# Modulation steps moved from two out-projections into the gMLP's u half, a PSUM bank held for a pair, a weight read moved ahead

## The chip, the cores and the metric

The kernel runs on one core of one Trainium2 chip. The metric is the device time of one execution in microseconds; less is better. A core has TensorE (PE, matmuls; PEld is its weight load), VectorE (DVE), ScalarE (ACT), GpSimd (POOL) and SyncE (SP, which here only issues DMAs). Each engine, and SP, works its instructions off in program order and waits on semaphores for the others.

## The reference

Two layers over 512 latent tokens and 256 context tokens, width 1024. Each layer is FFN, mixer, FFN; the mixer of the first layer is a chunked gMLP, that of the second is attention. Every sub-layer has shift, scale and gate vectors from a modulation of the conditioning, and ends in a layer norm.

```python
def modulation(cond, w_mod, b_mod):
    m = jax.nn.silu(cond) @ w_mod + b_mod
    return jnp.split(m[..., None, :], N_MOD, axis=-1)          # N_MOD = 9

def ffn_sublayer(x, shift, scale, gate, w_in, w_out, ln_g, ln_b):
    y = swiglu(modulate(x, shift, scale), w_in, w_out)
    return layer_norm(ALPHA * x + 0.5 * gate * y, ln_g, ln_b)

def gmlp_mix(h, w_in, sgu_g, sgu_b, w_s, b_s, w_out):
    b_, t_, _ = h.shape
    u, v = jnp.split(jax.nn.gelu(h @ w_in, approximate=False), 2, axis=-1)
    v = layer_norm(v, sgu_g, sgu_b)
    v = v.reshape(b_, t_ // CHUNK, CHUNK, GMLP_GROUPS, GMLP_HALF // GMLP_GROUPS)
    v = jnp.einsum('gpq,bnqgc->bnpgc', w_s, v) + b_s.T[None, None, :, :, None]
    return (u * v.reshape(b_, t_, GMLP_HALF)) @ w_out
```

## The kernel before

**Stages.** The six sub-layers run one after another; every one of the first five ends in an out-projection during which the next one's input is prepared. Times in the profiled execution: first FFN's gated products to 372 us, its out-projection to 554 and its end to some 580; the gMLP's v half to 754, its u half to 982, its out-projection to 1171; second FFN to 1679, third FFN to 2191, then attention and the last FFN.

**Products.** Operands are split into a high and a low part and each product takes three matmuls. Weights come by SP into six `raw` buffers; ScalarE rounds them to the high part, VectorE subtracts for the low part (`w`, eight buffers). The gated products and u use a Strassen scheme: seven products (B11, T1, T2, B21, T3, B22, T4; 12 matmuls each) for a pair of output chunks, partly added up by VectorE (`sums`). A product's end is a *slot*: `step` issues the product, then `slot` flushes the low parts that wait, prepares two more weight units (`pump`), runs a modulation step if asked to (`fills`), and then the evacuations (`post`).

**The u half** (`gmlp`). The twelve pairs are a loop over `a`. Its PSUM banks are four (`part_bank`); four more go round for the spatial products (`mix_bank`). The bank called `seeded` takes B11's copy, then T2, T3 and T4; after T4 ScalarE reads it in `gelu(x, seeded)`, behind two other GELUs. `b1` takes B11 and B21, `b2` takes T1 and B22. `bank()` gives out the bank that was given out longest ago and is not held. v is written to DRAM in the v half, read back chunk by chunk (`fetch`), normalised by ScalarE (`normed`) and multiplied by the group's spatial weights (`spatial`); VectorE scales the result into S (`mixed`) and multiplies it with u (`times`), one or two such jobs a slot from the list `late`. The products then go to DRAM by POOL (`act<-stage`) and come back for the out-projection (`q<-act`, by `feed` and `prepare`). `load_ws` reads a group's spatial weights.

**The modulation.** A unit (layer, i) is one of the nine vectors. It takes 16 steps (two halves of 512 columns by eight blocks of rows). A step (`fill`) is two instructions of VectorE (`acc<-mraw,cs,acc`, latent and context) on a 256 KB block of w_mod that SP loaded into one of three `mraw` buffers. After each half POOL sums over the partitions (`PARTITION_ALL_REDUCE`, L476) and adds the row to a DRAM vector (`mod<-acc`, L477), both conditions one after the other. When a shift and its scale are there, `mod_columns` reads them back (`s<-mod`) three steps later and has TensorE transpose them (`ps<-ident,s`) three steps after that; gates are read straight (`gate<-mod`). `MOD_PLAN` says in which sub-layer a unit's steps run; what is left at the end of an out-projection is drained there.

**The out-projection** (`out_proj`) goes through the chunks twice, once for each half of 512 output columns: 22 chunks in an FFN, 24 in the gMLP, 18 matmuls a chunk. Each chunk's slot has a weight unit, the next chunk's activations, and one or more `fill`s, whose rate `x % 8` and `acts.ring` (true in the gMLP) set. `residual` gives the jobs that bring the old stream into z; in the first sub-layer it is six plain loads. At the end each block of tokens is normalised: statistics on VectorE, the power -1/2 on POOL (L204), the scaling on ScalarE (L2239), transposes on TensorE.

The order of the work is the program order of these functions; when `pin` is on, VectorE and ScalarE keep it exactly.

Of the kernel before, what the change touches and what calls it, by code (L numbers as in the profile page):

```python
# [13 lines left out]
P = 128  # L14
# [12 lines left out]
GMLP_CH = GMLP_HALF // P  # L27
GMLP_GROUPS = 8
# [41 lines left out]
MOD_PLAN = [  # L70
    [(0, 2), (0, 3), (0, 4), (0, 5), (0, 6)],
    [(0, 7), (0, 8)],
    [(1, 0), (1, 1), (1, 2)],
# [21 lines left out]
class Backbone:  # L95
# [788 lines left out]
    def out_proj(self, acts, l, i, factor, end, prev, gate_at=2):  # L884
# [9 lines left out]
        for half, order in enumerate(orders):  # L894
            body = n - CLOSE * half
            for x in range(body):
# [22 lines left out]
                if adds:  # L919
                    if x:  # L920
                        b, z, tmp = adds.pop(0)
                        self.dve.tensor_tensor(z, z, tmp, ALU.add)
                        self.dve.bn_stats(st[b][:, 0], z)
                    self.fill(int(prev is None or self.light))
                elif residual and x > 2 and (half or x % 2):
                    residual.pop(0)()
                    self.fill(int(self.light or acts.ring and x % 4 == 1))
                elif half or x < n - 1:
                    self.fill_pair()
                    if prev is None and x % 8 in (1, 3, 6) or acts.ring and x % 8 in (2, 6):  # L930
                        self.fill()
# [494 lines left out]
    def gmlp(self, l, i, nblocks, end, prev):  # L1426
# [3 lines left out]
        vst = [self.const.tile([P, CC, 6], F32, name=f"vst{b}") for b in range(NB)]  # L1430
        room = self.box("v", F32)
        self.gmlp_v(room, spill, vst)
        dve, act = self.dve, self.act

        acts = Acts(self, GMLP_CH, TOK, KEPT_MIX, READ_BACK_MIX, f"act{l}{i}_")
# [5 lines left out]
        T1, T2 = slice(0, HT), slice(HT, TOK)  # L1441
        ws_raw = {}

        for x in range(4):
# [8 lines left out]
        def load_ws(g):  # L1453
            if g < GMLP_GROUPS:
                wg = ws_raw[g] = self.sm([P], "w_s")
                self.sp.dma_start(wg, io["gmlp_w_s"][0, g])

# [94 lines left out]
        nothing = lambda: None  # L1552
        load_ws(0)
        load_ws(1)
# [3 lines left out]
        for a in range(0, GMLP_CH, 2):  # L1558
            begin, final = not a, a == GMLP_CH - 2
            seeded = self.part_bank(marked=True)  # L1560
            b1, g = self.part_bank(), self.acc()[:, 0:HT]
            step(b1, "B11", False, lambda: act.copy(seeded, b1), v_stats if begin else lambda: normed(a))
            if begin:
                next(self.following)
            if final:
                self.filler_raw()
            b2, p5 = self.part_bank(), self.acc()[:, 0:HT]
            step(b2, "T1", False, None, lambda: act.copy(p5, b2), v_bias if begin else nothing)
            if final:
                acts.prepare(0, 0)  # L1570
            v, w = self.q(512)[:, 0:HT], self.q(512)[:, 0:HT]
            half = (lambda j, x: lambda: normed(j, range(HALF * x, HALF * x + HALF))) if begin else lambda j, x: nothing
            step(seeded, "T2", True, None, lambda: act.copy(v, seeded), half(0, 0))
            if final:
                acts.prepare(0, 1)
            step(b1, "B21", True, None, lambda: gelu(g, b1), half(0, 1))
            if begin:
                self.grp_next = next(self.following)
            else:
                spatial(a)  # L1580
                late.append(lambda: times(a, T1, g))
# [7 lines left out]
            if final:  # L1589
                acts.prepare(0, 2)  # L1590

# [4 lines left out]

            step(seeded, "T4", True, None, last)
            if begin:
# [742 lines left out]
```

## Time and profile before

| | us |
|---|---|
| three runs | 2809.52, 2812.65, 2814.51 (median 2812.65) |
| the profiled execution | 2813.58 |
| its span (first to last instruction) | 2811.8 |

| stage | us from the span's start | VectorE busy |
|---|---|---|
| first FFN, gated products with steps | 215 to 358 | 130.1 of 143.0 |
| its out-projection, four windows | 371.7 to 554 | 148.7 of 182.3 |
| u, eight pairs | 814.6 to 964.3 | 103.0 of 149.7 |

A row of the timeline has the start, the length, engine, line, operation, output and inputs, count, and in brackets the idle time of that engine before it with what ended it. L90 is the line of the wrapper through which most instructions are issued, so operations are told apart by the names of their tiles.

### The profile page before, as it was taken

The numbers are of one execution on the slowest core, as the hardware profiler recorded it, in microseconds if no ns is written. First come the engines' busy times: TensorE is split into PE (matmuls) and PEld (weight loads), VectorE is DVE, ScalarE is ACT, GpSimd is POOL, SyncE is SP. The second block draws the span as 40 slices with busy tenths as digits, with TensorE's granted clock in tenths as the row PEclk, the third lists the DMA queues.
The fourth block names the chain that finished last, engine by engine and source line by source line (L and its number), as shares of the span: only waits on it lengthen the run. The fifth ranks groups of instructions, "written<-read, shape, count | busy, mean of one in ns | idle before, by whom it ended". The sixth has DMA issues, their size and how long they took to land.

```text
span 2811.8 us, 40725 instructions
## 1 busy us (share of the span) xinstructions
PE 2737.7 (97%) x14234; PEld 2464.8 (88%) x14234; DVE 2086.1 (74%) x3554; ACT 1314.4 (47%) x2624; POOL 555.8 (20%) x627
## 2 busy tenths in 40 slices
PE   7999998999999999999999999999999999999998
PEld 5999986788899987899999889999988888888887
DVE  6879988777776687687898658789886598733445
ACT  6544432275566631474444237444432666623321
POOL 1002145312100143300223220013242121000001
PEclk9999999999999999999999999999999999999999
DMA  7444475457644584444546534454595524454352
GB/s 232 141 141 140 137 242 184 153 176 234 208 148 155 163 268 147 140 147 141 147 140 219 178 108 134 141 154 137 164 311 161 147 72 86 129 151 134 113 169 86
DMA packets 408134, 448.09 MB, mean 159 GB/s; under 512 B 29624, under 2 KB 289144, under 8 KB 407928
## 3 DMA queue, kind: packets, MB, share of 16 engines
q1 hardware_dynamic: 371416, 331.99, 38.2%
q0 software_dynamic: 36512, 113.51, 13.3%
q8 instruction: 111, 1.82, 0.3%
q14 instruction: 95, 0.78, 0.1%
HBM read 383.40 MB, written 64.19 MB: 159 GB/s over the span
## 4 chain that ended last, share of the span: by engine, by line
PE 78%; DVE 6%; issue 5%; ACT 4%; DMA 4%; POOL 3%; SPq 0%; DVEq 0%; POOLq 0%; ACTq 0%
PE ps L90 77%; POOL acc L476 2%; DVE acc L90 1%; DVE w L90 1%; DMA mraw<-in_w_mod_dram 1%; ACT w L90 1%; DMA q<-act 1%; PE pp L90 1%; DVE acts L90 1%; DMA raw<-in_w_mod_dram 1%; ACT z L2239 1%; DVE z L90 0%; DVE q L90 0%; ACT h L694 0%; DMA acc<-in_gmlp_w_in_dram 0%
## 5 line engine op out<-in xcount | busy, mean ns | idle before, releaser
L90 PE MATMUL ps<-comb,w 128*128 128x384 f32 x6552 | 1156.1, 336 | 11.4 <-ACT acc L90 5.8
L90 PEld LDWEIGHTS ps<-comb,w 128*128 128x128 f32 x6552 | 1137.8, 188 | 18.4 <-ACT acc L90 9.0
L90 PE MATMUL ps<-w,acts 128*128 128x512 f32 (+1 forms) x3792 | 867.7, 390 | 10.2 <-DVE q L90 8.1
L90 PEld LDWEIGHTS ps<-w,acts 128*128 128x128 f32 x3792 | 711.2, 189 | 158.7 <-DVE q L90 9.0
L90 ACT CAST w<-raw 128x512 fp32r<-128x512 f32 x643 | 397.7, 621 | 622.5 <-PE ps L90 520.0
L90 DVE TENSOR_TENSOR w<-raw,w 128x512 fp32r<-128x512 f32 x643 | 471.3, 738 | 284.7 <-ACT w L90 283.0
L90 DVE SCALAR_TENSOR_TENSOR acc<-mraw,cs,acc 128x512 f32<-128x512 f32 x392 | 277.7, 743 | 27.9 <-DMA mraw<-in_w_mod_dram 27.6
L476 POOL PARTITION_ALL_REDUCE acc<-acc x56 | 208.0, 3720 | 339.1 <-DVE acc L90 305.2
L90 PE MATMUL ps<-h,w 128*128 128x512 f32 (+1 forms) x1152 | 241.4, 372 | 0.2 <-DVE w L174 0.2
L90 POOL DMA_DIRECT2D act<-stage x86 | 48.1, 559 | 953.9 <-DVE stage L90 935.6
L90 PEld LDWEIGHTS ps<-h,w 128*128 128x128 f32 x1152 | 203.2, 188 | 37.7 <-DVE w L174 0.4
L90 DVE TENSOR_TENSOR w<-sums,w 128x512 fp32r<-128x512 f32 x234 | 165.3, 711 | 69.2 <-ACT w L90 69.0
L90 POOL DMA_DIRECT2D q<-act x234 | 134.1, 638 | 405.3 <-DVE acts L90 270.5
L90 ACT COPY q<-ps 128x384 f32<-128x384 f32 (+1 forms) x206 | 99.4, 483 | 237.3 <-PE ps L90 237.2
L90 ACT CAST acts<-q 128x384 fp32r<-128x384 f32 (+1 forms) x270 | 132.0, 520 | 98.2 <-DMA q<-act 80.4
L90 PE MATMUL ps<-w,comb 128*128 128x512 f32 x756 | 173.2, 390 | 0.4 <-DVE w L90 0.2
L90 DVE TENSOR_TENSOR acts<-q,acts 128x384 fp32r<-128x384 f32 (+1 forms) x270 | 160.2, 628 | 14.6 <-ACT acts L90 14.3
L90 PEld LDWEIGHTS ps<-w,comb 128*128 128x128 f32 x756 | 141.4, 188 | 30.9 <-DVE w L90 1.0
L90 ACT CAST w<-sums 128x512 fp32r<-128x512 f32 x234 | 144.8, 620 | 45.2 <-DVE sums L355 23.3
L90 DVE TENSOR_TENSOR q<-q,ps 128x384 f32<-128x384 f32 (+1 forms) x81 | 46.1, 570 | 58.7 <-PE ps L90 58.6
L204 POOL TENSOR_TENSOR rs<-ve,mhalf 128x1 f32<-128x1 f32 (+3 forms) x47 | 38.6, 821 | 249.3 <-DVE ve L201 139.6
L174 DVE TENSOR_TENSOR w<-raw,w 128x512 fp32r<-128x512 f32 x101 | 67.1, 687 | 25.2 <-ACT w L173 24.6
(208 smaller groups left out, 2491.3 us busy)
## 6 DMA issues: line engine op xcount, KB each, us to landing
raw<-in_ffn_w_in_dram SPq DMA_DIRECT2D x400, 256.0 KB
mraw<-in_w_mod_dram SPq DMA_DIRECT2D x256, 256.0 KB
raw<-in_ffn_w_out_dram SPq DMA_DIRECT2D x176, 256.0 KB
q<-act POOLq DMA_DIRECT2D x224, 192.0 KB, 4.6
raw<-in_gmlp_w_in_dram SPq DMA_DIRECT2D x132, 256.0 KB
act<-stage POOLq DMA_DIRECT2D x76, 384.0 KB, 3.2
zhat<-z POOLq DMA_DIRECT2D x26, 512.0 KB, 3.0
raw<-in_gmlp_w_out_dram SPq DMA_DIRECT2D x48, 256.0 KB
```

The costliest lines, as they stand in the source:

```text
L90: return self.tc.keep_in_program_order(f(*args, **kwargs))
L174: self.lows.append((key, lambda: self.dve.tensor_tensor(lo, src, hi.bitcast(F32), ALU.subtract)))
L204: self.last_rstd = self.nc.gpsimd.tensor_tensor(rs, ve, self.mhalf[:, 0:1].to_broadcast([P, n]), ALU.pow).ins
L476: nc.gpsimd.partition_all_reduce(accs[c], accs[c], P, bass_isa.ReduceOp.add)
L2239: k.act.activation(k.z[b], k.z[b], AF.Identity, bias=nb, scale=rs)
```

## The change

Unit (0, 6) moves from the first sub-layer's plan to the gMLP's. In the out-projection the extra steps are fewer: in the first sub-layer one extra at x % 8 == 3 instead of three in eight, in the gMLP none. In u, ten of the twelve pairs run a step in the slots of T1, B21 and B22, and three of those pairs one more in T4's. The bank of T4 is held until T4's slot is over (`part_bank("mixed")`, `unhold`). The temporaries g, p5 and x come from `q` and no longer from `acc`, which the modulation uses. The first group's spatial weights are read ahead of the v half. In the last pair the reads of the first activations for the out-projection are spread over three places.

```diff
 MOD_PLAN = [
-    [(0, 2), (0, 3), (0, 4), (0, 5), (0, 6)],
-    [(0, 7), (0, 8)],
+    [(0, 2), (0, 3), (0, 4), (0, 5)],
+    [(0, 6), (0, 7), (0, 8)],
...
                 elif residual and x > 2 and (half or x % 2):
                     residual.pop(0)()
-                    self.fill(int(self.light or acts.ring and x % 4 == 1))
+                    self.fill(int(self.light))
                 elif half or x < n - 1:
                     self.fill_pair()
-                    if prev is None and x % 8 in (1, 3, 6) or acts.ring and x % 8 in (2, 6):
+                    if prev is None and x % 8 == 3:
                         self.fill()
...
+        load_ws(0)
         self.gmlp_v(room, spill, vst)
...
-        def step(ps, name, go_on, early, *posts):
+        def step(ps, name, go_on, early, *posts, fills=0):
...
-            self.slot(post, 2, 0, early)
+            self.slot(post, 2, fills, early)
...
-        load_ws(0)
+        temp = lambda: self.q(512)[:, 0:HT]
         load_ws(1)
...
-            seeded = self.part_bank(marked=True)
-            b1, g = self.part_bank(), self.acc()[:, 0:HT]
+            seeded = self.part_bank("mixed", marked=True)
+            b1, extra = self.part_bank(), int(not begin and a < GMLP_CH - 2)
             step(b1, "B11", False, lambda: act.copy(seeded, b1), v_stats if begin else lambda: normed(a))
+            b2, p5 = self.part_bank(), temp()
+            step(b2, "T1", False, None, lambda: act.copy(p5, b2), v_bias if begin else nothing, fills=extra)
...
             if final:
-                self.filler_raw()
-            b2, p5 = self.part_bank(), self.acc()[:, 0:HT]
-            step(b2, "T1", False, None, lambda: act.copy(p5, b2), v_bias if begin else nothing)
-            if final:
                 acts.prepare(0, 0)
-            v, w = self.q(512)[:, 0:HT], self.q(512)[:, 0:HT]
+                acts.feed(0, 1)
+            v = temp()
...
-            step(b1, "B21", True, None, lambda: gelu(g, b1), half(0, 1))
+            g = temp()
+            step(b1, "B21", True, None, lambda: gelu(g, b1), half(0, 1), fills=extra)
...
-            if a >= GMLP_CH - 4:
-                acts.feed(0, 2)
+            w = temp()
             step(seeded, "T3", True, lambda: act.copy(w, seeded), half(1, 0) if begin else lambda: normed(a + 1))
-            step(b2, "B22", True, None, lambda: add(v, v, b2), lambda: add(w, w, p5), half(1, 1))
-            if not begin:
+            if final:
+                acts.prepare(0, 1)
+                acts.feed(0, 1)
+            step(b2, "B22", True, None, lambda: add(v, v, b2), lambda: add(w, w, p5), half(1, 1), fills=extra)
+            if begin:
+                self.filler_raw()
+            else:
                 spatial(a + 1)
-            x = self.acc()[:, 0:HT]
-            if final:
-                acts.prepare(0, 2)
+            if a == GMLP_CH - 4:
+                acts.feed(0, 1)
+            x = temp()
...
-            step(seeded, "T4", True, None, last)
+            step(seeded, "T4", True, None, last, fills=int(extra and a % 8 == 4))
+            self.unhold("mixed")
```

**How instructions move: SP in the first sub-layer's out-projection.** First the order before, at the place where the gate (`mod_1910`) and the columns of units (0, 3) and (0, 4) (`s_4470` from `mod_2930` and `mod_3862`) are read:

```order
L90 DMA mraw<-in_w_mod_dram 128x512 x2
L90 DMA raw<-in_ffn_w_out_dram 128x512
L90 DMA gate<-mod_1910 128x1024 x2
L90 DMA s_4470<-mod_2930 8x128
L90 DMA s_4470<-mod_3862 8x128
L90 DMA mraw<-in_w_mod_dram 128x512
```

The same place in the changed kernel, where the columns' tile is `s_4565`:

```order
L90 DMA gate<-mod_1910 128x1024 x2
L90 DMA mraw<-in_w_mod_dram 128x512
L90 DMA raw<-in_ffn_w_out_dram 128x512
L90 DMA mraw<-in_w_mod_dram 128x512
L90 DMA raw<-in_ffn_w_out_dram 128x512
L90 DMA mraw<-in_w_mod_dram 128x512
L90 DMA raw<-in_ffn_w_out_dram 128x512
L90 DMA s_4565<-mod_2930 8x128
L90 DMA s_4565<-mod_3862 8x128
```

The columns' read stood right behind the gate's two reads and now stands three chunks further on. In TensorE's order the transposes of these columns move with it, from behind 270 matmuls of the out-projection to behind 342.

**POOL at the end of the same sub-layer.** `mod_4852` is unit (0, 6) before; `mod_4453` in the change is unit (0, 5); `act_2` to `act_7` are the reads for the second pass, and L204 is the power for the closing layer norm:

```order
 L90 DMA q<-act_2_966 128x384 x2
 L90 DMA q<-act_3_967 128x384 x2
-L476 ISA acc<-acc 128x512
-L477 DMA mod_4852<-acc 16x1x32
-L476 ISA acc<-acc 128x512
-L477 DMA mod_4852<-acc 16x1x32
 L90 DMA q<-act_4_968 128x384 x2
 L90 DMA q<-act_5_969 128x384 x2
 L90 DMA q<-act_6_970 128x384 x2
 L90 DMA q<-act_7_971 128x384 x2
-L476 ISA acc<-acc 128x512
-L477 DMA mod_4852<-acc 16x1x32
-L476 ISA acc<-acc 128x512
-L477 DMA mod_4852<-acc 16x1x32
 L204 ISA
```

The last all-reduces stood directly ahead of L204; now none stands behind the read of act_2.

**VectorE in a pair of u.** Before, from the scaled bias (`s_`) of a pair's first spatial product, behind B21, to the additions behind B22 (`q<-q,ps`); `S` is the scaled spatial product, `w` a low part:

```order
L90 SCALAR_TENSOR_TENSOR s_7974<-S,sguT 128x128
L90 TENSOR_TENSOR w<-raw,w 128x512
L90 TENSOR_TENSOR w<-sums,w 128x512 x2
L355 TENSOR_TENSOR sums<-raw,sums 128x512
L90 TENSOR_TENSOR w<-raw,w 128x512
L90 SCALAR_TENSOR_TENSOR S<-ps,sguT,s_7974 128x384 x2
L90 TENSOR_TENSOR w<-raw,w 128x512
L336 TENSOR_TENSOR sums<-raw 128x512
L90 TENSOR_TENSOR q<-q,ps 128x384
L90 TENSOR_TENSOR q<-q,acc 128x384
```

The same stretch of a pair in the change:

```order
L90 SCALAR_TENSOR_TENSOR s_9165<-S,sguT 128x128
L90 TENSOR_TENSOR w<-sums,w 128x512 x2
L90 SCALAR_TENSOR_TENSOR acc<-mraw,cs,acc 128x512 x2
L90 TENSOR_TENSOR w<-raw,w 128x512
L90 SCALAR_TENSOR_TENSOR S<-ps,sguT,s_9165 128x384 x2
L355 TENSOR_TENSOR sums<-raw,sums 128x512
L90 SCALAR_TENSOR_TENSOR acc<-mraw,cs,acc 128x512 x2
L90 TENSOR_TENSOR w<-raw,w 128x512
L90 TENSOR_TENSOR q<-q,ps 128x384
L90 TENSOR_TENSOR q<-q 128x384
```

Two steps of the modulation (two `acc` instructions each) now stand in this stretch, those of the B21 and B22 slots; the third of the pair lies outside this piece. The additions read p5 from `q` and no longer from `acc`.

More of the change, by code (lines that the diff above doesn't have):

```diff
@@ L1431, in gmlp, with load_ws @@
         room = self.box("v", F32)
+        ws_raw = {}
+        def load_ws(g):
+            if g < GMLP_GROUPS:
+                wg = ws_raw[g] = self.sm([P], "w_s")
+                self.sp.dma_start(wg, io["gmlp_w_s"][0, g])
+        load_ws(0)
         self.gmlp_v(room, spill, vst)
@@ L1441, in gmlp @@
         T1, T2 = slice(0, HT), slice(HT, TOK)
-        ws_raw = {}
         for x in range(4):
@@ L1451, in mix_bank @@
             return self.psum.tile([P, 512], F32, tag=f"ps{x}", bufs=1, name="ps")
[L1453 to L1456, printed above, removed]
         def group(g):
@@ L1580, in gmlp @@
                 spatial(a)
-                late.append(lambda: times(a, T1, g))
-            if a >= GMLP_CH - 4:
-                acts.feed(0, 2)
+                late.append(lambda a=a, g=g: times(a, T1, g))
+            w = temp()
             step(seeded, "T3", True, lambda: act.copy(w, seeded), half(1, 0) if begin else lambda: normed(a + 1))
-            step(b2, "B22", True, None, lambda: add(v, v, b2), lambda: add(w, w, p5), half(1, 1))
-            if not begin:
+            if final:
[5 more added lines that the diff above has]
+            else:
                 spatial(a + 1)
-            x = self.acc()[:, 0:HT]
-            if final:
-                acts.prepare(0, 2)
+            if a == GMLP_CH - 4:
+                acts.feed(0, 1)
+            x = temp()
             def last():
@@ L1595, in last @@
                 gelu(x, seeded)
-            step(seeded, "T4", True, None, last)
+            step(seeded, "T4", True, None, last, fills=int(extra and a % 8 == 4))
+            self.unhold("mixed")
+            if final:
+                acts.prepare(0, 2)
             if begin:
```

1 line of the change is left out of this document (removed).

## The prediction

> **What bounds the kernel now.** I read the page's first part, then the waits of TensorE, then its timeline around each wait.
>
> ```profile
> PE 2737.7 (97%) x14234; PEld 2464.8 (88%) x14234; DVE 2086.1 (74%) x3554; ACT 1314.4 (47%) x2624; POOL 555.8 (20%) x627
> ...
> PE ps L90 <- DMA s<-mod: 11.9, 1, 11.9
> PE ps L90 <- DVE q L90: 8.1, 2, 4.6
> PE ps L90 <- ACT acc L90: 6.0, 11, 0.6
> PE ps L90 <- ACT z L2239: 5.3, 1, 5.3
> PE ps L90 <- DMA s<-in_gmlp_w_s_dram: 3.5, 1, 3.5
> PE ps L90 <- DVE acts L90: 1.8, 1, 1.8
> ```
>
> TensorE is busy 97% of the span and the change leaves its work alone, so the change can only win the few places where TensorE stands still: the rows give total, number of times, longest. All but part of the 8.1 lie between 400 and 1090 us, where the change is. These are the places in the timeline (start, length, last in brackets the idle time before):
>
> ```profile
> 406.82 28.52 PE L90 MATMUL ps<-w,acts 128*128 128x512 f32 x124 [1.81 <-DVE acts L90]
> 447.23 0.28 PE L90 MATMUL ps<-ident,s 32*128 32x32 f32 x1 [11.88 <-DMA s<-mod]
> 559.23 1.97 PE L90 MATMUL ps<-ident,z 128*128 128x128 f32 x8 [5.29 <-ACT z L2239]
> 759.68 0.33 PE L90 MATMUL ps<-ident,s 128*128 128x128 f32 x1 [3.45 <-DMA s<-in_gmlp_w_s_dram]
> 843.12 4.41 PE L90 MATMUL ps<-comb,w 128*128 128x384 f32 x24
> 847.37 1.98 PE L90 MATMUL ps<-zraw,v 128*128 128x128 f32 x12
> 849.10 2.34 PE L90 MATMUL ps<-comb,w 128*128 128x384 f32 x12
> 852.02 8.59 PE L90 MATMUL ps<-comb,w 128*128 128x384 f32 x48 [0.58 <-ACT acc L90]
> 1087.07 13.20 PE L90 MATMUL ps<-w,acts 128*128 128x512 f32 x47 [4.58 <-DVE q L90]
> ```
>
> A long wait costs more than itself. The windows (engines in the order of the page, with instructions; behind POOL the granted clock) show it:
>
> ```profile
> 448.00:452.00 4.00, 4.00 (x11) 3.10 (x10) 3.53 (x6) 0.00 (x0) 0.76 (x2) 0.50 0.77 251
> 450.50:454.00 3.50, 3.50 (x10) 2.69 (x9) 3.50 (x5) 0.00 (x0) 2.72 (x3) 0.56 0.82 242
> 460.00:464.00 4.00, 4.00 (x19) 3.32 (x18) 4.00 (x9) 1.37 (x4) 1.00 (x2) 1.00 0.43 132
> 559.20:563.00 3.80, 3.77 (x14) 3.34 (x15) 1.25 (x5) 2.61 (x6) 1.33 (x3) 0.53 0.34 138
> 759.60:763.00 3.40, 3.32 (x14) 3.32 (x15) 0.77 (x2) 0.78 (x2) 1.22 (x1) 0.67 1.04 289
> 1088.00:1091.00 3.00, 3.00 (x8) 2.32 (x7) 2.68 (x5) 0.00 (x0) 3.00 (x1) 0.50 0.06 1
> ```
>
> After the 11.88 us wait the clock is 0.50 and 4 us hold 11 matmuls instead of 19, so 42% of that time is lost; the 0.56 of the next row puts the return to full clock near 453.6, some 6.2 us after the wait: 2.6 us. The same arithmetic (share 0.42) gives 1.5 behind the 5.29 wait (0.53 in its row: half clock for about 3.6 us), 1.4 behind the 3.45 wait and 2.0 behind the 4.58 wait (I take 3.4 and 4.8 us of half clock there).
>
> **The change, part by part.**
>
> *First layer's first out-projection, 1.8 + 11.9 + 2.6 = 16.3 us.* Why did the columns come late?
>
> ```profile
> 395.62 2.74 DVE L90 SCALAR_TENSOR_TENSOR acc<-mraw,cs,acc 128x512 f32<-128x512 f32 x4 [9.10 <-DMA mraw<-in_w_mod_dram]
> 422.40 5.20 POOL L476 PARTITION_ALL_REDUCE acc<-acc  x1 [1.18 <-DVE acc L90]
> 432.24 0.80 POOL L477 DMA_DIRECT2D mod<-acc  x1 [0.30 <-POOL acc L476]
> 435.54 0.85 SPq L90 DMA_DIRECT2D gate<-mod  x2
> 436.55 2.64 SPq L90 DMA_DIRECT2D s<-mod  x4
> ```
>
> VectorE lost 9.1 us to a late weight of w_mod, so the last all-reduce for unit (0,4) began only at 422.4 and its row left at 432.2; SP issued the columns' read at 436.6, directly behind the gate, and it was in at 447.2. TensorE had reached the transposes at 435.3. They stand behind 15 chunks of 18 matmuls before and behind 19 after (270 and 342 in its order), and a chunk takes 18 x 4/19 = 3.8 to 28.52/124 x 18 = 4.1 us: 4 chunks move them 15 to 16.5 us later. The mod steps come at a lower rate, one or two a chunk as before but two only at x % 8 == 3, so the all-reduce moves back too, by about two chunks (8 us), though VectorE then lags less. Against an 11.9 us wait that leaves 15 + (the gate no longer ahead, 2 rows) - 8: near zero. I take the wait as gone and keep 2 us for a rest. VectorE's part per chunk falls too, which is what the 1.8 us waited for.
>
> *End of the same sub-layer, 5.3 + 1.5 = 6.8 us.* The wait is for the first block's normalisation:
>
> ```profile
> 549.51 0.80 POOL L477 DMA_DIRECT2D mod<-acc  x1 [0.30 <-POOL acc L476]
> 550.97 0.15 DVE L201 TENSOR_SCALAR ve<-mv 128x1 f32<-128x1 f32 x1
> 557.12 0.59 POOL L204 TENSOR_TENSOR rs<-ve,mhalf 128x1 f32<-128x1 f32 x1 [6.81 <-issue]
> 1171.05 1.03 PE L90 MATMUL ps<-ident,z 128*128 128x128 f32 x8
> ```
>
> Its input was ready at 551.1, but POOL had just finished unit (0,6)'s all-reduce and spent 6.8 us before the power (POOL's order has an ISA instruction at L204 there, at the first power behind an all-reduce). Without (0,6) the last all-reduce stands before the reads of act_2 to act_7, six chunks ahead, so the 6.8 us lie beside matmuls. The next sub-layer's end (row at 1171.05) has no wait.
>
> *Spatial weights ahead of v, 3.5 + 1.4 = 4.9 us.* One 64 KB DMA on SP moves ahead of all of v. What could be late next is the read of v from its spill, issued at the same place in SP's order; I keep 0 to 3 us for it and take 0.
>
> *gMLP's out-projection, 4.6 + 2.0 = 6.6 us.* It held 32 mod steps, now 15. VectorE worked 42.4 of 46 us ahead of the wait:
>
> ```profile
> 1030.00:1076.00 46.00, 46.00 (x204) 38.10 (x203) 42.40 (x65) 16.97 (x34) 20.30 (x22) 1.00 0.75 245
> 379.38 2.72 DVE L90 SCALAR_TENSOR_TENSOR acc<-mraw,cs,acc 128x512 f32<-128x512 f32 x4
> ```
>
> A step is two such instructions, 2.72/4 = 0.68 us each; 17 steps fewer take 23 us off VectorE in some 180 us. The backlog goes, and with it the wait.
>
> *The held bank in u, up to 8.0 us.* From the timeline above, T4's products start at 849.10 and the next at 852.02, 2.92 us, where a product elsewhere takes (847.37 - 843.12)/2 = 2.12. That 0.8 us comes ten times. With the bank held, the next B11 goes to a bank that was emptied long before.
>
> *What u has to pay.* u gets 33 steps in ten pairs (three each, four in three of them), and eight all-reduces with their DMAs on POOL.
>
> ```profile
> 814.62:964.30 149.68, 145.04 (x880) 140.80 (x880) 102.97 (x190) 95.15 (x221) 10.80 (x20) 1.00 0.46 145
> 215.00:358.00 143.00, 143.00 (x825) 142.70 (x824) 130.09 (x201) 67.05 (x133) 30.62 (x21) 1.00 0.49 140
> 264.64 2.73 DVE L90 TENSOR_TENSOR w<-raw,w 128x512 fp32r<-128x512 f32 x1
> 267.30 0.68 DVE L355 TENSOR_TENSOR sums<-raw,sums 128x512 f32<-128x512 f32 x1
> 267.90 0.68 DVE L90 TENSOR_TENSOR w<-raw,w 128x512 fp32r<-128x512 f32 x1
> ```
>
> Eight pairs hold 103.0 us of VectorE, 12.9 each. The steps add 66 x 0.68 = 45 us to ten pairs. Each all-reduce stretches one instruction of VectorE by 2.73 - 0.68 = 2.05 us: 16 us. Sum 129 + 45 + 16 = 190 us, against TensorE's 10 x (18.7 - 0.8) = 179. Packed instructions start 0.60 apart and not 0.68 (last two rows), which takes the 129 to 114 and the sum to 175. So VectorE would be between 4 us short of TensorE and 11 us beyond it. In the first FFN's gated part (row at 215) VectorE was busy 91% and TensorE never stood, so some lag is absorbed; here it is 98 to 106%. I charge 5 us, towards the middle. Below nothing isn't possible: nothing leaves VectorE in u. The added w_mod loads (33 x 256 KB over 180 us, 47 GB/s beside 145) have room. On SP they now stand between u's weights and the reads of v, and each waits until VectorE frees its buffer, with the next weights behind it; eight w buffers, of which a step uses one, cover some 12 us of that. At u's end POOL has the read of act_0 behind two all-reduces (3.4 to 5.2 us each by the rows above), and ScalarE's queue holds that cast ahead of T2's copy: nothing to 5 us, I take 2, since the read needs some 14 us from the step that frees it and TensorE has 14.5 us of work until T3.
>
> [...]
>
> **The sum.** The profiled execution took 2813.6 us (span 2811.8 and 1.8 around it), 0.9 above the median. Gains 16.3 + 6.8 + 4.9 + 6.6 + 8.0 = 42.6; charges 5 (u) + 2 (its end) + 2 (rest of the columns' wait) = 9. 2813.6 - 42.6 + 9 = **2780**.
>
> **Rivals.**
> - *VectorE becomes the bound in u.* Unpacked instructions (190 us) and an all-reduce that takes VectorE for its whole 3.45 us (8 x 1.4 = 11 more) make 201 against 179: 22 us instead of 5, about 2797. For it: 98 to 106% load; b2's bank is now reused every pair, so TensorE's T1 waits for VectorE's add about 6 us after B22. Against: no wait in the row at 215. Chance 0.14. [...]
> - *The columns' wait stays*, since the burst of z loads ahead of the late w_mod weight is untouched: half of 11.9 + 2.6 back, 2780 + 6 = 2786, or all of it, 2793. Chance 0.10.
> - *Slower:* w_mod weights come late to VectorE inside u as at 395.62. Its queue is in order, so weights' low halves, sums and bank evacuations stand behind the waiting step. It turns the sign when a pair loses over 4 us (42.6 + 5.6 over ten pairs, less what is charged); at 9.1 us a pair, 4 of them absorbed, it is 51 us: about 2822. Against: a DMA share of 0.46 in u, where that wait fell in one of 0.83. Chance 0.05.
> - *Nothing measurable*, u giving back all that the rest wins: 0.05.
>
> **Numbers.** Forecast 0.66 (2770 to 2790; all gains, no charge: 2771). The range goes to 2800, over the first two rivals. A measurement tells about 0.2% (5.6 us) from no change. Faster 0.66 + 0.14 + 0.10 = 0.90, same 0.05, slower 0.05.
>
> **What would show it.** In the waits of TensorE: no s<-mod, z, w_s, no 4.6 for q; no 0.58 for ScalarE at each pair. VectorE near full from 790 to 970 and, if I am wrong there, rows of TensorE <- DVE or ACT at T1, T3 or the spatial products. A wait for s<-mod of over 3 us, or a pair in u of over 19 us, makes the prediction wrong.

## The result and the profile after

| | before | after |
|---|---|---|
| median of four runs, us | 2811.09 (2807.66 to 2814.51) | 2791.76 (2789.83 to 2794.73) |
| the profiled execution, us (span) | 2813.58 (2811.8) | 2794.73 (2792.9) |
| ratio of the times | | 0.9932, 95% interval 0.9915 to 0.9949 |

The changed kernel is 0.7% faster: 18.9 us between the two profiled spans, where 33.6 had been worked out. Every stage can be compared, since TensorE runs the same products in the same order. The start of a stage here is the start of the same matmul in both traces:

| stage | before, us | after, us | difference | predicted |
|---|---|---|---|---|
| up to the first out-projection | 371.7 | 373.4 | +1.7 | 0 |
| first out-projection, to the chunk behind its second block's transposes | 195.0 | 173.2 | -21.8 | -21.1 |
| to the v half | 31.5 | 31.9 | +0.4 | 0 |
| v half | 155.7 | 157.9 | +2.2 | 0 |
| u, first pair | 23.2 | 21.7 | -1.5 | -4.9 |
| u, ten pairs | 187.2 | 189.6 | +2.4 | -3.0 |
| u, last pair | 17.8 | 18.5 | +0.7 | +2.0 |
| gMLP's out-projection | 189.7 | 186.1 | -3.7 | -6.6 |
| from there to the end | 1640.0 | 1640.6 | +0.7 | 0 |

The rows +1.7, +0.4 and +0.7 lie where the change touches nothing; the four runs of one kernel differ by up to 6.9 us. A stage's time comes from one execution. The ten pairs of u repeat well: two kernels below that have the same work there take 178.7 us each, and the changed kernel and one other 189.6 and 189.7. The gMLP's out-projection repeats less well: with the same code it took 189.7 us in the kernel before and 185.4 and 188.5 in those first two kernels.

In the page of the changed kernel the engines' busy times are what they were (TensorE 2737.7 and 2735.2, VectorE 2086.1 and 2085.0); its first line, and then rows of the waits of TensorE (total, times, longest):

```profile
PE 2735.2 (98%) x14234; PEld 2464.5 (88%) x14234; DVE 2085.0 (75%) x3554; ACT 1313.8 (47%) x2624; POOL 554.2 (20%) x627
```

```profile
PE ps L90 <- DVE q L90: 6.9, 3, 3.2
PE ps L90 <- ACT q L90: 6.4, 5, 2.0
PE ps L90 <- DVE S L90: 4.2, 2, 3.2
PE ps L90 <- ACT ps L90: 2.0, 2, 1.4
```

The rows for `s<-mod` (11.9), `z` (5.3), the spatial weights (3.5) and `acc` (6.0) are gone. The rows for `S`, for ScalarE's `q` and for ScalarE's `ps` are new. TensorE's timeline shows where:

```profile
373.38 78.00 PE L90 MATMUL ps<-w,acts 128*128 128x512 f32 x342
451.30 0.24 PE L90 MATMUL ps<-ident,s 32*128 32x32 f32 x1
467.26 73.73 PE L90 MATMUL ps<-w,acts 128*128 128x512 f32 x324 [1.88 <-DVE q L90]
545.80 1.03 PE L90 MATMUL ps<-ident,z 128*128 128x128 f32 x8
655.09 41.11 PE L90 MATMUL ps<-w,comb 128*128 128x512 f32 x180 [1.40 <-ACT ps L90]
756.84 1.62 PE L90 MATMUL ps<-zraw,v 128*128 128x128 f32 x6 [3.22 <-DVE S L90]
817.92 8.09 PE L90 MATMUL ps<-comb,w 128*128 128x384 f32 x36 [1.76 <-DVE q L90]
903.62 4.46 PE L90 MATMUL ps<-comb,w 128*128 128x384 f32 x24 [1.80 <-ACT q L90]
970.49 36.60 PE L90 MATMUL ps<-w,acts 128*128 128x512 f32 x153 [2.02 <-ACT q L90]
1151.49 1.03 PE L90 MATMUL ps<-ident,z 128*128 128x128 f32 x8
```

342 matmuls run without a break ahead of the columns' transposes, and the transposes wait for nothing; so do the z transposes at 545.80. Within u, where ten waits of 0.58 us have gone, VectorE and ScalarE are now waited for in some pairs. The windows of the changed kernel show how full VectorE is over the ten pairs (third pair of numbers), and the clock behind four of the waits:

```profile
758.10:947.70 189.60, 182.89 (x1102) 179.53 (x1102) 171.30 (x294) 118.81 (x275) 44.39 (x35) 0.99 0.62 186
```

```profile
758.10:762.10 4.00, 4.00 (x20) 4.00 (x20) 1.85 (x4) 0.69 (x2) 0.57 (x1) 0.75 0.84 254
818.00:822.00 4.00, 4.00 (x14) 4.00 (x15) 4.00 (x9) 4.00 (x10) 0.00 (x0) 0.57 0.35 95
903.62:907.62 4.00, 4.00 (x23) 4.00 (x24) 4.00 (x9) 2.55 (x7) 0.56 (x1) 1.00 0.57 176
970.40:974.40 4.00, 3.92 (x12) 3.13 (x13) 4.00 (x9) 3.44 (x8) 0.83 (x2) 0.67 0.42 124
```

VectorE's own waits in the same stretch:

```profile
DVE sums L336 <- DMA raw<-in_gmlp_w_in_dram: 12.7, 8, 3.3
DVE w L90 <- ACT w L90: 5.5, 5, 2.4
```

171.3 busy, 12.7 waiting for u's weights and 5.5 for ScalarE make 189.5 of 189.6 us. The wait for ScalarE is the time in which VectorE has nothing to do, and little of it is left. The same rows of the kernel before, over its ten pairs:

```profile
DVE w L90 <- ACT w L90: 50.4, 35, 2.5
DVE sums L336 <- DMA raw<-in_gmlp_w_in_dram: 5.4, 9, 0.8
```

There VectorE waited 50.4 us for ScalarE to give it work, which is slack, and only 5.4 us for weights.

What a lag looks like: VectorE from 894 us, two all-reduces on POOL beside it, and ScalarE behind it.

```profile
894.11 1.13 DVE L90 SCALAR_TENSOR_TENSOR S<-ps,sguT,s 128x384 f32<-128x384 f32 x2
895.16 1.91 DVE L90 TENSOR_TENSOR w<-raw,w 128x512 fp32r<-128x512 f32 x1
896.99 1.01 DVE L90 TENSOR_TENSOR stage<-q,S 128x384 f32<-128x384 f32 x2
897.93 0.74 DVE L90 SCALAR_TENSOR_TENSOR acc<-mraw,cs,acc 128x512 f32<-128x512 f32 x1
898.59 0.68 DVE L90 TENSOR_TENSOR w<-raw,w 128x512 fp32r<-128x512 f32 x1
899.19 2.69 DVE L90 TENSOR_TENSOR stage<-q,S 128x384 f32<-128x384 f32 x1
901.80 0.68 DVE L339 TENSOR_TENSOR sums<-sums,raw 128x512 f32<-128x512 f32 x1
```

```profile
894.29 3.23 POOL L476 PARTITION_ALL_REDUCE acc<-acc  x1 [11.55 <-DVE acc L90]
898.98 3.49 POOL L476 PARTITION_ALL_REDUCE acc<-acc  x1
```

```profile
902.57 0.62 ACT L90 CAST w<-sums 128x512 fp32r<-128x512 f32 x1 [4.20 <-DVE sums L339]
903.09 0.47 ACT L90 COPY q<-ps 128x384 f32<-128x384 f32 x1
```

Two of VectorE's instructions take 1.91 and 2.69 us instead of 0.69 and 0.55. The sum of L339 is then late, ScalarE stands 4.20 us for it, and the copy of T2, next in ScalarE's queue, comes 1.80 us too late for T3 on TensorE (the row at 903.62). No single wait here is long; the lag is handed on from queue to queue.

### The profile page after: what moved, and what is told of

The parts are those of the page before. It is cut to its first block, busy times and chain, and to the rows that moved or that the text cites. A ratio compares the mean times of both kernels' runs of the same rounds, so it can differ in the third digit from the quotient of the medians.

```text
span 2792.9 us, 40728 instructions
## 1 busy us (share of the span) xinstructions
PE 2735.2 (98%) x14234; PEld 2464.5 (88%) x14234; DVE 2085.0 (75%) x3554; ACT 1313.8 (47%) x2624; POOL 554.2 (20%) x627
## 4 chain that ended last, share of the span: by engine, by line
PE 58%; DVE 2%; ACT 2%; issue 2%; POOL 1%; DMA 1%; SPq 0%; DVEq 0%; POOLq 0%; ACTq 0%
PE ps L90 57%; PE pp L90 1%; POOL acc L476 1%; ACT h L694 0%; ACT z L2244 0%; POOL rs L204 0%; ACT p L1758 0%; DMA mraw<-in_w_mod_dram 0%; DMA q<-act 0%; DVE z L90 0%; DVE nm L1750 0%; DVE w L90 0%; ACT w L173 0%; ACT comb L708 0%; DVE q L90 0%
## 5 line engine op out<-in xcount | busy, mean ns | idle before, releaser
L90 PE MATMUL ps<-comb,w 128*128 128x384 f32 x6552 | 1155.4, 336 | 11.7 <-ACT q L90 4.4
L90 DVE TENSOR_TENSOR w<-raw,w 128x512 fp32r<-128x512 f32 x643 | 476.8, 746 | 291.1 <-ACT w L90 289.7
L90 DVE TENSOR_TENSOR acts<-q,acts 128x384 fp32r<-128x384 f32 (+1 forms) x272 | 153.7, 602 | 12.2 <-ACT acts L90 12.2
L204 POOL TENSOR_TENSOR rs<-ve,mhalf 128x1 f32<-128x1 f32 (+3 forms) x47 | 38.6, 820 | 273.6 <-DVE ve L201 170.7
L174 DVE TENSOR_TENSOR w<-raw,w 128x512 fp32r<-128x512 f32 x101 | 67.2, 688 | 25.6 <-ACT w L173 25.1
```

Source lines behind the costliest of these rows:

```text
L90: return self.tc.keep_in_program_order(f(*args, **kwargs))
L174: self.lows.append((key, lambda: self.dve.tensor_tensor(lo, src, hi.bitcast(F32), ALU.subtract)))
L204: self.last_rstd = self.nc.gpsimd.tensor_tensor(rs, ve, self.mhalf[:, 0:1].to_broadcast([P, n]), ALU.pow).ins
```

## The experiments

Each ratio is to the kernel before on the same chip, with its 95% interval; stages are those of the table above.

**The held bank alone**, on the kernel before:

```diff
-            seeded = self.part_bank(marked=True)
+            seeded = self.part_bank("mixed", marked=True)
...
             step(seeded, "T4", True, None, last)
+            self.unhold("mixed")
```

> The kernel before with one edit: the bank of a pair's last product is held to the pair's end; no modulation step in u. My term (T4's wait of 0.58 us and its 0.2 us of start disappear ten times): the ten pairs of u take 187.2 - 8.0 = 179.2 us and the whole kernel is 8 us shorter, ratio 0.997. Rival (with the bank held, the bank of the product that VectorE adds up comes back every pair, and T1 waits for that add even without steps): the ten pairs take 183 to 187 us, TensorE's rows show waits for VectorE at T1, and the kernel is 0 to 4 us shorter.

Ratio 0.9969 (0.9958 to 0.9980), 2805.0 us. The ten pairs take 178.7 instead of 187.2 us: 8.4 us, and TensorE waits for nothing in them. The term is right, and the rival is out: without steps T1 never waits for the addition.

**The early spatial weights alone**, on the kernel before: `load_ws(0)` ahead of `gmlp_v`, as in the change.

> The kernel before with one edit: the first spatial weights are read ahead of v. My term: the 3.45 us wait and 1.4 us of slow clock behind it are gone and nothing is late in their place, 4.9 us shorter; then the 2.2 us that v lost in the changed kernel, in waits for ScalarE's evacuations, have another cause and do not show here. Rival (the early read, or the buffer that it holds through v, is what costs v 2.2 us): v takes 157.9 instead of 155.7 us with waits for ScalarE of 0.6 to 1.4 us, and the kernel is 2.7 us shorter. If the wait of 3 us in u's first pair for VectorE's copy of the spatial sums shows here too, it is not due to the first step.

Ratio 0.9991 (0.9982 to 1.0000): 2.5 us, between 0 and 5. That is the total of the rival, though 4.9 is only at the edge; the rival's reason, a slower v, falls with the next run. Only its times are read; the stages come from the next run.

**Both together:**

> The kernel before with the held bank and the early spatial weights together, no step in u. If the two add: 8.4 + 2.5 = 11 us shorter, ratio 0.996. The profile splits the second term: the 3.45 us wait for the weights goes, a wait of about 2.4 us for VectorE's copy of the spatial sums comes in the first pair without any step, and v takes 1 us longer. If the first pair has no such wait here, it came with the changed kernel's buffers for temporaries.

Ratio 0.9966 (0.9954 to 0.9977). The v half takes 155.3 us, so the early weights do not slow v down. The first pair takes 19.7 instead of 23.2 us, and this row of TensorE's timeline stands in it:

```profile
773.31 0.91 PE L90 MATMUL ps<-zraw,v 128*128 128x128 f32 x6 [1.83 <-DVE S L90]
```

The wait for VectorE's copy of the spatial sums is there without any step and with the old buffers: it is what was late next behind the weights. 3.5 us of the 4.9 are won in the pair; the total gained only a little over the held bank's, within the intervals.

**The steps without the hold**, the changed kernel less `"mixed"` and `unhold`:

> The changed kernel with the bank of T4 not held any more; the steps stay in u. If VectorE (busy or waiting for weights all through the ten pairs of u) is what sets their length, the hold is worth nothing there: they stay at 189 to 191 us and the kernel at its time, ratio to before 0.993. If the steps are a cost beside TensorE's work, as the prediction summed them, the hold is worth its 8.4 us here too: 198 us and a kernel 8 us longer, ratio 0.996.

Ratio 0.9943 (0.9929 to 0.9958). The ten pairs take 199.4 us, 9.8 more than in the changed kernel. The theory that VectorE's work alone sets the length of u falls: then the hold would have been worth nothing. TensorE's rows here show what the hold does beside saving 0.6 us a pair:

```profile
792.15 8.59 PE L90 MATMUL ps<-comb,w 128*128 128x384 f32 x48 [0.64 <-ACT q L90]
815.76 10.69 PE L90 MATMUL ps<-comb,w 128*128 128x384 f32 x48 [5.56 <-ACT q L90]
```

Where ScalarE lags, the wait for T4's bank grows to 5.56 us, and the matmuls behind it are slower (48 in 10.69 us instead of 8.59). In the changed kernel, where the bank is held, no wait for it is left.

**No steps in u:** units (0, 6) and (0, 7) at the old rate in the gMLP's out-projection, (0, 8) in the FFN behind.

```diff
-    [(0, 6), (0, 7), (0, 8)],
-    [(1, 0), (1, 1), (1, 2)],
+    [(0, 6), (0, 7)],
+    [(0, 8), (1, 0), (1, 1), (1, 2)],
...
-            b1, extra = self.part_bank(), int(not begin and a < GMLP_CH - 2)
+            b1, extra = self.part_bank(), 0
```

> The changed kernel with no modulation step in u: units (0,6) and (0,7) run in the gMLP's out-projection at the rate of the kernel before, unit (0,8) in the FFN behind it; the pair's temporaries stay in six q buffers and the bank stays held. If steps and all-reduces are what u paid for (10.4 us over ten pairs against the held bank's 179.2): the ten pairs take 179 to 180 us, the first pair loses its 3.2 us wait, the out-projection gets 3 to 6 us back as waits for q, and the kernel takes 2791.8 - 10.4 - 4 + 5 = about 2782 us. If the temporaries' buffers (six instead of ten) are what u paid for: the ten pairs stay at 186 to 189 us with T3 waiting for ScalarE's copy to q, and the kernel takes 2788 to 2793 us. The 16 steps in the FFN behind cost 0 to 3 us in both.

The ten pairs take 180.3 us without a wait (the 1.6 above the held bank's 178.7 lies behind a wait of 2.4 us at the end of the first pair, with a clock of 0.66 over the 4 us from 752.70), so the six buffers for temporaries cost nothing and the steps and all-reduces are what u pays for. The rest of the expectation was wrong: 2819.1 us, ratio 1.0016 (1.0008 to 1.0025). The FFN behind did not take 16 more steps for 0 to 3 us; what was left was drained at its end, in front of the z transposes:

```profile
1682.48 1.97 PE L90 MATMUL ps<-ident,z 128*128 128x128 f32 x8 [28.48 <-ACT z L2244]
```

The out-projection took 195.5 us, with waits for VectorE of 6.3 us and for the columns of 2.7. The 33 steps have to go somewhere, and u is not the worst place.

**No all-reduces in u:**

```diff
+                if (l, i) not in ((0, 6), (0, 7)):
-                nc.gpsimd.partition_all_reduce(accs[c], accs[c], P, bass_isa.ReduceOp.add)
+                    nc.gpsimd.partition_all_reduce(accs[c], accs[c], P, bass_isa.ReduceOp.add)
```

> The changed kernel without the partition all-reduces of units (0,6) and (0,7), eight in u; their rows are then one partition's sum and not the sum of all. If it is the all-reduces (each holds VectorE for about 2 us more in the one instruction that it meets): the ten pairs of u fall from 189.5 to 180-182 us and the kernel by 8 to 10 us, to 2783. If it is the steps' own 45 us of VectorE in a queue that is full: the pairs fall by a quarter of 10.4 us, to 186-187, the kernel to 2788. If it is the temporaries' buffers: 188.5 to 189.5 us, the kernel as it was.

Ratio 0.9876 (0.9864 to 0.9889), 2779.1 us. The ten pairs take 181.4 us, and the out-projection behind them 182.9. Steps without all-reduces cost u next to nothing. The transfers of w_mod are all still there, so they are not the price either. And u's weights are as late as in the changed kernel: VectorE waits 11.7 us for them, while TensorE waits just once in the ten pairs, 0.5 us.

```profile
756.10:937.50 181.40, 180.89 (x1103) 178.25 (x1102) 162.54 (x300) 118.86 (x275) 20.85 (x34) 0.99 0.66 197
DVE sums L336 <- DMA raw<-in_gmlp_w_in_dram: 11.7, 9, 3.3
```

What the all-reduces change is when VectorE comes to such a wait. The longest one of both kernels lies at the same place, around the start of the fourth of the ten pairs. These are SP's three loads ahead of it and the wait itself, first of the changed kernel, then of this one:

```profile
800.94 8.35 SPq L90 DMA_DIRECT2D mraw<-in_w_mod_dram  x3
816.71 0.69 DVE L336 TENSOR_TENSOR sums<-raw 128x512 f32<-128x512 f32 x1 [3.33 <-DMA raw<-in_gmlp_w_in_dram]
```

```profile
798.06 5.77 SPq L90 DMA_DIRECT2D mraw<-in_w_mod_dram  x3
811.26 0.69 DVE L336 TENSOR_TENSOR sums<-raw 128x512 f32<-128x512 f32 x1 [3.35 <-DMA raw<-in_gmlp_w_in_dram]
```

The wait is as long in both, but TensorE began the pair at 813.91 in the changed kernel and at 811.17 here, so it ends 2.8 us into the pair there and 0.1 us here. In the changed kernel T1 then waits for VectorE's addition (the row at 817.92) and the pair takes 21.6 us; here it takes 18.0.

**All-reduces without the products:**

```diff
+                    if k and (l, i) in ((0, 6), (0, 7)):
+                        continue
                     if k:
                         dve.scalar_tensor_tensor(accs[c], raw, cs, accs[c], ALU.mult, ALU.add)
```

> The changed kernel with the eight all-reduces and all w_mod transfers in u, but without 28 of the 32 steps' products of units (0,6) and (0,7) (only the first weight of each half is multiplied); VectorE has 38 us less to do and SP waits for none of it. If an all-reduce costs TensorE about 1 us by itself: the ten pairs take 179 + 8 = 187 us. If all-reduces cost only where VectorE is already behind, with the steps and u's late weights ahead of it: they take 180 to 182 us. The wait of 2.4 to 3.2 us for the spatial sums in the first pair stays in both.

Ratio 0.9873 (0.9857 to 0.9890). The ten pairs take 179.8 us: eight all-reduces (one of them already in the first pair) cost TensorE nothing by themselves either. Each lasts 3.2 to 3.5 us and lengthens VectorE's instructions beside it by 0 to 2.0 us, against the usual length of the same instruction. In the changed kernel, where they last 3.2 to 5.9 us, it is 0.6 to 3.3 us, 14.8 us for the eight, which last 31.3 us together: less than half of their length. TensorE waits for nothing over the ten pairs here, where VectorE has few products beside them; in the changed kernel, where it has all of them, TensorE waits 6.7 us.

**Half the steps:** 16 steps and four all-reduces in u, the rest in the out-projection at the old rate.

```diff
-            step(b1, "B21", True, None, lambda: gelu(g, b1), half(0, 1), fills=extra)
+            step(b1, "B21", True, None, lambda: gelu(g, b1), half(0, 1), fills=int(extra and a % 4 == 0))
...
-            step(b2, "B22", True, None, lambda: add(v, v, b2), lambda: add(w, w, p5), half(1, 1), fills=extra)
+            step(b2, "B22", True, None, lambda: add(v, v, b2), lambda: add(w, w, p5), half(1, 1))
...
-            step(seeded, "T4", True, None, last, fills=int(extra and a % 8 == 4))
+            step(seeded, "T4", True, None, last, fills=int(a == 12))
```

> The changed kernel with 16 steps and four all-reduces in u instead of 33 and eight; units (0,7) and (0,8) run in the gMLP's out-projection again at the rate of the kernel before. If the cost in u grows with the steps and all-reduces (10.8 us for all of them): the ten pairs take 184 us; if there is a threshold, at which VectorE is full, half of them cost 0 to 1.5 us: 179 to 180.5 us. The out-projection takes 185 to 189 us, as before the change or as in the held-bank run, instead of 186. The kernel is 3 to 9 us shorter, ratio 0.990 to 0.992.

Ratio 0.9900 (0.9884 to 0.9917). The ten pairs take 185.1 us, 6.4 above the held bank's: half of the load costs more than half of the price, with VectorE busy in only 149.9 of 185.1 us. So it is no threshold of the mean load; but VectorE waits 11.7 us for u's weights here too. Most of the price is one place. After two all-reduces at 848.0 and 852.9 a step comes late, SP stands at the loads that wait for it, VectorE then waits 4.24 us for u's weights, and T3 comes 2.12 us late, with slower matmuls behind it (24 in 6.03 us, where 4.43 is usual):

```profile
852.40 7.24 SPq L90 DMA_DIRECT2D mraw<-in_w_mod_dram  x2
866.37 0.69 DVE L336 TENSOR_TENSOR sums<-raw 128x512 f32<-128x512 f32 x1 [4.24 <-DMA raw<-in_gmlp_w_in_dram]
877.98 6.03 PE L90 MATMUL ps<-comb,w 128*128 128x384 f32 x24 [2.12 <-ACT q L90]
```

The out-projection takes 186.6.

**The weights of w_mod issued later.** In the changed kernel SP issues the next block of w_mod right behind the step that frees its buffer, and stands there until VectorE has done the step. Here it is issued one step later, in u only:

```diff
-                self.filler_raw()
+                if not self.lazy:
+                    self.filler_raw()
...
             begin, final = not a, a == GMLP_CH - 2
+            self.lazy = not final
```

> The changed kernel with each w_mod weight in u issued one step later, when the buffer that it goes to has long been read, so that SP does not stand at it with u's own weights behind it. Theory: VectorE is full in u because it also stands 12.7 us for u's weights (5.4 us in the kernel before), and that comes from SP's queue: the waits for raw fall to 5 to 7 us, the ten pairs from 189.5 to 182-185 us, the kernel by 5 to 7 us, ratio 0.991. Rival (the w_mod transfers themselves make u's weights late, or VectorE's work is what counts): raw waits stay over 10 us, the pairs at 188 to 190, ratio 0.993.

Ratio 0.9894 (0.9879 to 0.9908), 2784.6 us; ten pairs 185.1, out-projection 182.9. SP's row for the three loads that held it 8.35 us in the changed kernel (the row at 800.94 above):

```profile
798.45 2.10 SPq L90 DMA_DIRECT2D mraw<-in_w_mod_dram  x3
```

Over the ten pairs SP waits 3.9 us for VectorE's steps, where it waited 50.8 in the changed kernel. And VectorE's wait for u's weights in this run is 1.4 us where the changed kernel had 12.7:

```profile
DVE sums L336 <- DMA raw<-in_gmlp_w_in_dram: 1.4, 3, 0.6
```

**All-reduces apart.** The second condition's last product of a half, and with it its all-reduce, comes one step behind the first's, with the weights issued at once as in the change (but for the block behind the divided step, which comes with the next one). Dividing takes one more call of `fill` a unit; so here and in the next run u has 34 calls, which do the 32 steps of two units, where the changed kernel does 33:

```diff
+                split = k == KD - 1 and (l, i) in ((0, 6), (0, 7))
+                part(0)
+                if nconds > 1 and not split:
+                    part(1)
...
+            send(0)
+            if split:
+                def carry(part=part, send=send):
+                    part(1)
+                    send(1)
```

> The changed kernel with the two all-reduces of a half one step apart in u, and the w_mod weights issued at once as in the changed kernel (the fourth of four: neither 189.6 us for the ten pairs, late issue alone 185.1, both 180.7). If VectorE's lag behind two all-reduces in a row is what TensorE feels and SP's standing only adds to it: 182 to 184 us, about what the late issue does not win. If late weights for u are the larger half by themselves: 185 to 188 us with raw waits of over 10 us. Ratio 0.989 to 0.992.

Ratio 0.9891 (0.9875 to 0.9908), ten pairs 186.3 us, VectorE's wait for weights 9.9. That is the second forecast's time, though its wait was to be over 10.

**Both, later weights and all-reduces apart:**

> The kernel with late-issued w_mod weights, and in u the second condition's last product and all-reduce one step (some 6 us) behind the first's, so that no two all-reduces run back to back. If it is the two in a row (some 4 us of VectorE lost within 8 us) that TensorE feels: the ten pairs take 180 to 182 us instead of 185.1 and the kernel 2780 us, ratio 0.988. If each all-reduce has its price alone: 184 to 186 us, ratio 0.9894.

Ratio 0.9874 (0.9859 to 0.9888), 2778.4 us: the fastest complete kernel of the study, 0.6% below the changed one by the ratios, whose intervals do not meet. The intervals of the three mended kernels overlap, so it is the ten pairs, each from one execution, that tell these apart:

| | all-reduces in a row | apart |
|---|---|---|
| w_mod issued at once | 189.6 | 186.3 |
| issued one step later | 185.1 | 180.7 |

Each mends its part (3.3 and 4.5 us), and together they mend 8.9. This run's ten pairs and VectorE's waits in them:

```profile
752.70:933.37 180.67, 180.67 (x1103) 178.44 (x1102) 171.91 (x297) 118.93 (x275) 43.38 (x38) 0.99 0.62 194
```

```profile
DVE w L90 <- ACT w L90: 6.0, 7, 2.1
DVE sums L336 <- DMA raw<-in_gmlp_w_in_dram: 2.2, 2, 1.6
```

VectorE is busy 95% of the window, and TensorE 100%. The steps and all-reduces run in u almost without a price, 1.9 us over the held bank alone.

**The first pair**, with the first three w_mod blocks issued earlier:

```diff
             if begin:
                 next(self.following)
+                self.filler_raw()
...
-            if begin:
-                self.filler_raw()
-            else:
+            if not begin:
                 spatial(a + 1)
```

> The changed kernel with the first three weights of w_mod issued one product after B11 of u's first pair, five products earlier. If the first step, late for its weight with the copy of the spatial sums behind it, made the 3.2 us wait in the first pair: that wait is gone, the pair takes 18.5 instead of 21.7 us and the kernel is 3 to 4 us shorter, ratio 0.992. Rival (VectorE is late there for u's own weights, which wait on SP in either order): the wait moves but stays over 2 us, and the kernel gains under 1 us.

Ratio 0.9914 (0.9899 to 0.9928). By the total the theory would stand, though the interval overlaps that of the changed kernel; by the profile it falls: the wait for `S` is 4.2 us, and the pair takes 22.7. Of the 6.7 us between the two profiled spans 3.2 lie in the out-projection (182.9) and 2.5 ahead of the first out-projection, and the edit touches neither. Over the runs that wait is 1.8 us with neither steps nor new buffers, 2.4 with the buffers alone, 2.2 to 4.2 with steps or their transfers; why it differs so among these was not settled.

## Why the prediction was right, and where it fell short

The direction and the range held, and the terms outside u were found: 2780 was forecast, 2791.76 measured. That is little more than half of the forecast gain, and it lies within the range because the range had been stretched to 2800 for two rivals. Of the 14.7 us between the forecast and the measured span 5.4 lie in the ten pairs, 3.4 in the first pair, 2.9 in the gMLP's out-projection and 2.2 in v. The ten pairs even have the wrong sign, +2.4 for -3.0. Of the prediction's own signs of being wrong one came: three of the ten pairs take over 19 us (21.6, 19.6 and 20.0), so its account of u was wrong, though its total was in range. Point by point:

- **First out-projection and its end: right.** -21.8 against -23.1 and 2 kept for a rest. No wait for `s<-mod` or `z` is left, though VectorE still lost 8.5 us to a late block of w_mod (9.1 before), which was the second rival's reason. The 2 us came as something else, the wait of 1.88 us at 467.26 for VectorE, at the change of halves; that the row fits this closely is in part luck.
- **The held bank: right**, 8.4 for 8.0, shown alone and, with 9.8, under the load of the steps.
- **Spatial weights: the wait was found, what is late next was not.** "I keep 0 to 3 us for it and take 0" named the read of v; late next is VectorE's copy of the spatial sums, 1.8 us without the steps and 3.2 with them. That takes 3.4 of the 4.9 us, and another 0.9 at the start of the ten pairs (0.75 of the clock in the row at 758.10; 48 matmuls in 9.50 us instead of 8.57).
- **u: mis-sized, and weighed by the wrong measure.** The charge of 5 us came from a sum of VectorE's time against TensorE's, 175 to 190 against 179. VectorE's busy time, 171.3, lay even below the packed end, and the all-reduces' part of it was right (14.8 us for 16), and u still paid 10.9 us (189.6 against 178.7). Against the u without steps (180.3), steps alone cost 1.1 us (181.4) and all-reduces alone nothing (179.8), but both together 9.3; 4.5 of these went when SP no longer stood, 3.3 when the all-reduces were apart. The sentence that failed is that each w_mod load "waits until VectorE frees its buffer, with the next weights behind it; eight w buffers [...] cover some 12 us of that", which put this wait at nothing in the sum. VectorE itself waited 12.7 us for those weights, 7.3 more than before. Without the all-reduces it waited 11.7 us, and TensorE felt that in one wait of 0.5 us; with them VectorE came to the longest of these waits 2.7 us later in the pair, behind 8.35 us of SP at the three loads instead of 5.77, and the two added up. The chain from all-reduce to step, to SP, to weights, to TensorE is to be seen at one place in the run with half the steps; that every part of the 9.3 us goes this way is not shown.
- **The rival of VectorE as the bound** is half right: its signs were there (T1 behind the addition, the row at 817.92, with 0.57 of the clock behind it), but not its reason, unpacked instructions and all-reduces that block for their whole length: VectorE lost 14.8 us beside eight all-reduces that last 31.3, where the rival took 8 x 3.45, and with the same work it was busy 171.9 of 180.7 us in the run with both mends, where TensorE was busy in all of them. What it left out are VectorE's own waits for weights. In the six runs that have 32 or 33 steps in u and the held bank, the ten pairs take 5.6 to 7.4 us more than VectorE's busy time and these waits together:

| | busy | waits for weights | sum | ten pairs |
|---|---|---|---|---|
| both mends | 171.9 | 2.2 | 174.1 | 180.7 |
| no all-reduces | 162.5 | 11.7 | 174.2 | 181.4 |
| later weights | 176.3 | 1.4 | 177.7 | 185.1 |
| all-reduces apart | 170.7 | 9.9 | 180.6 | 186.3 |
| changed kernel | 171.3 | 12.7 | 184.0 | 189.6 |
| early blocks in the first pair | 171.1 | 11.8 | 182.9 | 189.7 |

That is a reading of the runs and not a test, and it is not the whole: with half the steps the sum is 161.6 and the pairs take 185.1.

- **u's end: 2 us forecast, nearer 4.** The last pair lost 0.7, and the out-projection's first chunks 2.0 in the wait at 970.49 with some 1.2 of half clock (0.67). In five runs (no all-reduces, no products, early blocks, later blocks, both mends) the wait there is 0.5 us at most and the out-projection takes 182.9. Why it is longer in the changed kernel was not settled.
- **gMLP's out-projection: the wait is gone as forecast, the size is less sure.** It is -6.8 (189.7 to 182.9) where it starts in time, for the 6.6 forecast; in the changed kernel 3.2 of that are lost to the late start above. But with the code of the kernel before the stage also took 185.4 and 188.5 us (its wait for VectorE 3.0 and 3.4 us instead of 4.6), so the gain is 2.5 to 6.8 us.
- **v: not forecast.** The runs with the changed first out-projection have v at 156.1 to 157.9, those without at 155.3 to 156.3. The early weights are not the cause. In the changed kernel POOL stands 2.32 us between two of the loads that add up v's weights, for nothing that the profile shows, as it did not in the kernel before. Why, and whether that is all of it, is open.

```profile
641.38 1.78 POOL L90 DMA_DIRECT2D acc<-in_gmlp_w_in_dram  x2 [2.32 <-issue]
```

## What to carry to other kernels

A sum of busy times says whether the work fits, not whether it fits in time: put beside it what the engine will wait for its own loads, the longest burst that it meets, and what stands behind it in the other queues. Loads that were issued right behind the instruction that frees their buffer held the DMA queue for 50.8 us over the ten pairs here; issued one step later they held it for 3.9 us, and the wait for the other loads fell from 12.7 to 1.4 us. Here it also paid to spread a burst by one step (186.3 us for the ten pairs instead of 189.6) before moving the work to another stage.

## What the runs showed of the hardware

- Two loads that cost u 1.1 us and nothing by themselves cost 9.3 us together: 33 steps (181.4 us for the ten pairs), eight all-reduces (179.8), both (189.6), against 180.3 with neither.
- The granted clock fell behind some short waits of TensorE and not behind others: 0.57 over the 4 us behind a wait of 1.76 us (817.92), 1.00 behind one of 1.80 (903.62). What decides it was not shown.
